# Fourteen weight splits of the output projection are taken from VectorE and given to transfers that GpSimd issues

## The chip, the cores and the metric

The kernel runs on one NeuronCore of a Trainium2 chip. The metric is the device time of one execution in microseconds (us). Before the change it was 1078.8 us, the median of two runs (1078.34 and 1079.26).

## The reference

One layer of a streaming encoder on 512 frames of 2048 columns. A combined input projection feeds two groups of heads, an RWKV-7 scan (16 heads of 64) and an HGRN2 recurrence (8 heads of 128). Their gated outputs are put side by side and go through one output projection, and a LayerNorm closes the layer:

```
proj   = x @ w_in                                  # 512 x 2048 by 2048 x 8320
o_rwkv = group_norm(rwkv7_scan(...)) ... * silu(z)  # 512 x 1024
o_hgrn = rms_norm(hgrn2_chunkwise(...)) * silu(z)   # 512 x 1024
y      = concat([o_rwkv, o_hgrn]) @ w_out           # 512 x 2048 by 2048 x 2048
out    = layer_norm(ALPHA * x + y) * ln_w + ln_b
```

The change touches only how the weights of the product with `w_out` are made ready.

## The kernel before, in words

**Products of two parts.** Every large product is made from float32 numbers that are cut in two. The high part is the number rounded to the short format of TensorE's fast pass (float32r), the low part is what is left. One product is then three matmuls: high by high, low by high and high by low (`three`, L426). `split` (L390) makes the parts: ScalarE writes the high part with an `ACTIVATE` copy, then VectorE subtracts it from the raw number and writes the low part.

**The output projection.** The 2048 output columns are taken in four blocks `d` of 512. A block runs over 16 contraction steps of 128 rows. The weights of one step, 128 partitions by 512 columns (256 KB in float32), are a *quarter*. For each quarter the four row tiles `t` of the output take three matmuls each, so a quarter keeps TensorE for twelve matmuls. Blocks 0 and 1 go through `rows`, blocks 2 and 3 through code of their own. The left operands `gh`, `gl` (tiles `xh`, `xl`) are the split gated head outputs. While block 0 runs, the last two HGRN2 heads are still being finished, and their matmuls (tile `mix`, L317 and L321) stand between the matmuls of the quarters. In block 1 only quarters are left.

**Buffers.** Raw weights come from `w_all` in halves, two quarters in one transfer of 512 KB that SyncE issues (`load`, L405) into one of two `wr` buffers. A new half is asked for once both quarters of the half two places before are split. High parts live in three `wh` buffers and low parts in three `wl` buffers. So quarter j+2 can be made ready as soon as TensorE has used up quarter j-1, that is when quarter j begins; and it must be ready when quarter j+2 begins.

**The order of the work.** The program is written by a planner at build time (`Plan`). Every operation is an `Op` with an engine, an estimated cost, and the tiles that it reads and writes. Queues of generators are pumped between matmuls, and the planner's clock decides which comes next. What comes out is one fixed order for each engine; at run time each engine goes through its own list in order, and semaphores hold an instruction until what it needs is there. `ready(i, home)` makes the split of quarter i and queues it; `part` holds TensorE's program until the planner's clock says that the low part is there. GpSimd (POOL) does little in this part of the program: four small power operations (`rsqrt`, L372) on `sm` and `rs`, for the heads.

Of the kernel before, what the change touches and what calls it, by code (L numbers as in the profile page):

```python
# [7 lines left out]
F32 = mybir.dt.float32  # L8
F32R = mybir.dt.float32r
U8 = mybir.dt.uint8  # L10
AF = mybir.ActivationFunctionType
ALU = mybir.AluOpType
# [222 lines left out]
def mixer_kernel(ctx, tc, head, x_r, w_all, par, up, ln_wb, consts, hmask, out):  # L235
    nc = tc.nc
    pe, sc_e, dve, pool = nc.tensor, nc.scalar, nc.vector, nc.gpsimd
# [17 lines left out]
    plan = Plan({**BUFS, **PBUFS})  # L255
    tags = {}

    def st(tag, shape, dt=F32):
        return spool.tile(shape, dt, tag=tag, name=nm(tag), bufs=BUFS[tag])
# [67 lines left out]
    def act_way(o, i, f, scale=1.0, bias=0.0):  # L327
        cost = 0.09 + size(o) * 0.00085 + moved(o, i) + (0.06 if isinstance(scale, bass.AP) else 0.0)
        if f == AF.Copy:
            return "act", cost, lambda: sc_e.activation(o, i, f, scale=scale)  # L330
        return "act", cost, lambda: sc_e.activation(o, i, f, scale=scale, bias=bias)  # L331

    def act(o, i, f, scale=1.0, bias=0.0):
        return Op([act_way(o, i, f, scale, bias)], [i], [o], SETS.get(f))
# [4 lines left out]
    def tt(o, a, b, f=ALU.mult):  # L339
        return dve_op([a, b], o, lambda: dve.tensor_tensor(o, a, b, f),  # L340
                      base=0.16 if o.shape[0] < P and size(o) == C and o.tensor.name in tags else 0.07)
# [48 lines left out]
    def split(hi, lo, raw):  # L390
        yield act(hi, raw, AF.Copy)
        yield tt(lo, raw, hi.bitcast(F32), ALU.subtract)
# [5 lines left out]
    raws, parts = {}, {}  # L398

    FIRST = 3  # L400
    nhead = 2 * FIRST
    nload = w_all.shape[0] + nhead
    QT = HALF // 2

    def load(j):  # L405
        if j < nload:
            raws[j] = st("wr", [P, HALF])
            nc.sync.dma_start(raws[j], w_all[j - nhead])
            plan.fetched(raws[j], 4 * HALF)

    whole_parts = set()

    def ready(i, home=None):

        if i < 2 * nload and i not in parts:
            parts[i] = home() if home else tuple(st(t, [P, QT], F32R) for t in ("wh", "wl"))

            def run():
                yield from split(*parts[i], raws[i // 2][:, i % 2 * QT : i % 2 * QT + QT])
                whole_parts.add(i)  # L420
                if i % 2:
                    load(i // 2 + 2)

            plan.add(splits, run())
# [16 lines left out]
    def part(i, width):  # L441

        ready(i)
        hi, lo = parts[i]
        plan.until(lambda: i in whole_parts and by_now(lo))
        return (hi.rearrange("p (k c) -> p k c", c=width), lo.rearrange("p (k c) -> p k c", c=width))
# [10 lines left out]
    def proj(u, hook=None):  # L457

        ps = main_ps()
        for j in range(4):  # L460
            if hook:
                hook(j)
            hi, lo = part(4 * u + j, P)
            for kk in range(4):
                if kk == 1:
                    ready(4 * u + j + 1)
                if kk == 2:
                    ready(4 * u + j + 2)
                k = 4 * j + kk
                three(ps, hi[:, kk], lo[:, kk], xh[k], xl[k], k == 0, k == KT - 1)  # L470
        return ps

    def rows(q, width, lh, ll, fin, order=range(KT), hook=None, tags=("main",)):

        pss = []
        per = QT // width
        for j in range(KT // per):
            if hook:
                hook(j)
            hi, lo = part(q + j, width)  # L480
            for t in range(4):
                if j == 0:
                    pss.append(main_ps(tags)[:, :width])
                if 0 < t < 3:
                    ready(q + j + t)
                sl = slice(t * P, t * P + P)
                for kk in range(per):
                    n = j * per + kk
                    k = order[n]
                    three(pss[t], lh[k][:, sl], ll[k][:, sl], hi[:, kk], lo[:, kk], n == 0, n == KT - 1)  # L490
                if j == KT // per - 1:
                    fin(t, pss[t])

    nunit = [0]

    def unit(n=1):
        u = nunit[0]
        nunit[0] += n
        return u
# [739 lines left out]
    for name, j in _order()[1:]:  # L1239
        if name == "i":  # L1240
# [7 lines left out]
            def fin(t, ps, ia=ia, j=j, used=used):  # L1248
                def run():
                    if t == 0:  # L1250
                        yield room(ia=1)
                        ia.append(take("ia", [P, 4, T]))
                    yield copy(ia[0][:, t], ps)
                    drop(ps)
                    if t == 3:
                        for S in HS[4 * j : 4 * j + 4]:
                            S.update(i=ia[0], used=used)

                plan.add(evacs, run())
# [140 lines left out]
    def ahead(j, d):  # L1400

        if d == 0:
            split_gated(j + 2)
            if j == 8:
                plan.until(room(big=1))
                lnw.append(take("big", [P, 2, D]))
                nc.sync.dma_start(lnw[0], ln_wb[None].to_broadcast([P, 2, D]))
                plan.fetched(lnw[0], 8 * D)
        if 0 <= j - KT // 2 - 3 < 4:
            residual(j - KT // 2 - 3, d)  # L1410

    banks = ("main", "acc", "mix")
    for d in range(2):
        rows(4 * unit(4), T, gh, gl, lambda t, ps, d=d: fin(t, ps, d), korder, lambda j, d=d: ahead(j, d),
             banks if d else banks[:1])
# [7 lines left out]
    def home(n):  # L1423
        if n < 10:
            return lambda: tuple(take("t", (P, QT), F32R) for _ in range(2))
        if n == 10:
            return lambda: tuple(take("ksq", (P, QT), F32R) for _ in range(2))
        if n < 13:
            def both():
                if not homes:  # L1430
                    homes["ia"] = take("ia", (P, 4, QT), F32R)
                return homes["ia"][:, 2 * (n - 11)], homes["ia"][:, 2 * (n - 11) + 1]

            return both
# [7 lines left out]
    for j in range(KT):  # L1442
        ahead(j, 2)
        hi, lo = part(q0 + seq.index((2, j)), T)
# [9 lines left out]
    for t in range(4):  # L1454
        sl = slice(t * P, t * P + P)
        ps = main_ps(banks)
        for n, k in enumerate(korder):
# [4 lines left out]
            hi, lo = part(q0 + seq.index((3, n)), T)  # L1462
# [81 lines left out]
```

## Time and profile before

| | before |
|---|---|
| median of two runs | 1078.8 us |
| the profiled execution | 1079.05 us |
| its span, first to last instruction | 1077.2 us |
| mean granted TensorE clock | 0.996 |
| TensorE busy | 1064.5 us, 99% of the span |
| VectorE busy | 771.2 us, 72% |
| ScalarE busy | 456.8 us, 42% |
| GpSimd busy | 63.7 us, 6% |

The profile is of one execution. PE is TensorE, PEld its weight loads, DVE is VectorE, ACT ScalarE, POOL GpSimd, SP SyncE. Matmuls overlap in the pipeline, so a matmul is listed with some 390 ns although the next starts 227 ns after it; the pace is read from the starts. In a row of the timeline the columns are start in us, duration in us, engine, line, operation, output and inputs (numbers of buffers left out), tile sizes, count, and in brackets the idle time before it and what ended it. In a row of transfers the columns are output and input, issuing queue, operation, count, size and the median time from issue to landing.

### The profile page before, as it was taken

Reading aid. Unit: us, or ns where it says so; the run is one execution under the profiler, and the core shown is the slowest. Engines: PE = TensorE matmul, PEld = TensorE weight load, DVE = VectorE, ACT = ScalarE, POOL = GpSimd, SP = SyncE. Lnnn points to the kernel's source line nnn. Section 1 sums busy time; section 2 is a strip of 40 time slices with the busy share of each in tenths; the row PEclk is TensorE's granted clock in tenths of the full one; section 3 lists DMA queues with packets and bytes.
Section 4 is the critical chain, followed back from the end, with each engine's and each line's share of the span. In section 5 each row is a group of like instructions: output and inputs, shape, how many; then the busy total and the mean of one; then the engine's idle time right before and its main releaser. Section 6 shows DMA issues by size and latency. Waiting matters only on the chain.

```text
span 1077.2 us, 18772 instructions
## 1 busy us (share of the span) xinstructions
PE 1064.5 (99%) x7210; PEld 889.8 (83%) x7210; DVE 771.2 (72%) x1816; ACT 456.8 (42%) x1015; POOL 63.7 (6%) x145
## 2 busy tenths in 40 slices
PE   9999999999999999999999999999999999999995
PEld 7888888888888888888888888888888888888884
DVE  6478978776679678787986776566976887625456
ACT  6443354544332456444236353434346564323321
POOL 0001000010000000011000001001000001000000
PEclk9999999999999999999999999999999999999998
DMA  8222321222323222123332223233332244545613
GB/s 324 62 90 78 98 80 61 63 91 89 108 75 108 87 69 76 55 93 98 92 99 61 79 60 93 89 82 105 89 98 60 61 147 153 175 122 166 204 60 127
DMA packets 34937, 108.47 MB, mean 101 GB/s; under 512 B 4128, under 2 KB 5664, under 8 KB 34720
## 3 DMA queue, kind: packets, MB, share of 16 engines
q1 hardware_dynamic: 34704, 107.08, 31.9%
q8 instruction: 57, 0.93, 0.4%
q14 instruction: 32, 0.26, 0.1%
q10 hardware_dynamic: 144, 0.20, 0.1%
HBM read 99.92 MB, written 7.34 MB: 100 GB/s over the span
## 4 chain that ended last, share of the span: by engine, by line
PE 98%; DVE 1%; DMA 0%; ACT 0%; SPq 0%; issue 0%; DVEq 0%
PE main L431 72%; PE mix L317 10%; PE mix L431 4%; PE acc L431 4%; PE main L1153 3%; PE acc L317 3%; PE mix L321 3%; PE main L317 1%; DMA q<-head 0%; DVE inv L349 0%; DVE inv L340 0%; SPq L1123 0%; DVE stats L1376 0%; ACT xh L330 0%; DVEq L1540 0%
## 5 line engine op out<-in xcount | busy, mean ns | idle before, releaser
L431 PE MATMUL main<-xh,wh 128*128 128x512 f32 x864 | 342.6, 397 | 0.0
L431 PE MATMUL main<-xl,wh 128*128 128x512 f32 x864 | 342.1, 396 | 0.0
L431 PE MATMUL main<-xh,wl 128*128 128x512 f32 x864 | 341.7, 396 | 0.0
L330 ACT ACTIVATE wh<-wr 128x512 fp32r<-128x512 f32 x299 | 186.6, 626 | 204.2 <-PE main L431 159.5
L340 DVE TENSOR_TENSOR wl<-wr,wh 128x512 fp32r<-128x512 f32 x299 | 203.9, 683 | 85.0 <-ACT wh L330 83.4
L431 PEld LDWEIGHTS main<-xh,wl 128*128 128x128 f32 x864 | 162.5, 188 | 32.2
L431 PEld LDWEIGHTS main<-xl,wh 128*128 128x128 f32 x864 | 162.6, 188 | 31.9
L431 PEld LDWEIGHTS main<-xh,wh 128*128 128x128 f32 x864 | 162.6, 188 | 31.5
L431 PE MATMUL main<-wh,xl 128*128 128x512 f32 x256 | 102.4, 400 | 0.0
L431 PE MATMUL main<-wh,xh 128*128 128x512 f32 x256 | 101.5, 396 | 0.0
L431 PE MATMUL main<-wl,xh 128*128 128x512 f32 x256 | 101.3, 396 | 0.0
L330 ACT ACTIVATE z<-mix 64x64 f32<-64x64 f32 (+1 forms) x153 | 35.9, 235 | 66.7 <-PE mix L317 27.3
L431 PEld LDWEIGHTS main<-wl,xh 128*128 128x128 f32 x256 | 48.2, 188 | 9.5
L431 PEld LDWEIGHTS main<-wh,xl 128*128 128x128 f32 x256 | 48.2, 188 | 9.1
L431 PEld LDWEIGHTS main<-wh,xh 128*128 128x128 f32 x256 | 48.2, 188 | 9.0
L331 ACT ACTIVATE t<-main,om 128x512 f32<-128x512 f32 x33 | 22.4, 688 | 73.6 <-PE main L431 64.0
L382 DVE COPY z<-mix 64x64 f32<-64x64 f32 (+1 forms) x167 | 37.8, 226 | 17.1 <-PE mix L317 8.2
L349 DVE SCALAR_TENSOR_TENSOR bd<-mix,pc,bd 64x64 f32<-64x64 f32 x112 | 31.3, 283 | 20.7 <-PE mix L317 15.0
L340 DVE TENSOR_TENSOR inv<-inv,inv 64x30 f32<-64x30 f32 (+14 forms) x120 | 38.6, 322 | 3.8 <-DVE inv L340 0.5
L349 DVE SCALAR_TENSOR_TENSOR t<-main,pr,t 128x511 f32<-128x511 f32 x33 | 24.3, 745 | 23.5 <-ACT t L331 23.3
L340 DVE TENSOR_TENSOR inv<-inv 64x30 f32<-64x30 f32 (+14 forms) x120 | 38.5, 321 | 2.9
L340 DVE TENSOR_TENSOR t<-t,tot 128x256 f32<-128x256 f32 x96 | 37.7, 415 | 0.3
(228 smaller groups left out, 1469.0 us busy)
## 6 DMA issues: line engine op xcount, KB each, us to landing
wr<-w_all SPq DMA_DIRECT2D x156, 512.0 KB, 3.6
q<-head SPq DMA_DIRECT2D x15, 448.0 KB, 5.6
g<-x_r SPq DMA_DIRECT2D x16, 256.0 KB, 3.9
spill<-g SPq DMA_DIRECT2D x12, 256.0 KB, 3.1
out<-q SPq DMA_DIRECT2D x12, 256.0 KB, 2.6
t<-spill SPq DMA_DIRECT2D x11, 256.0 KB, 4.0
big<-ln_wb SPq DMA_DIRECT2D x1, 2048.0 KB, 9.2
up<-up SPq DMA_DIRECT2D x8, 128.0 KB, 2.1
```

Of the source, the lines that this page charges most:

```text
L317: return Op([("pe", cost, lambda: pe.matmul(o, l, r, start=start, stop=stop, **kw))], [l, r], [o], mode="narrow" if narrow else "main" if ...
L321: return Op([("pe", 0.11, lambda: pe.transpose(o, i, ident))], [i], [o])
L330: return "act", cost, lambda: sc_e.activation(o, i, f, scale=scale)
L331: return "act", cost, lambda: sc_e.activation(o, i, f, scale=scale, bias=bias)
L340: return dve_op([a, b], o, lambda: dve.tensor_tensor(o, a, b, f), base=0.16 if o.shape[0] < P and size(o) == C and o.tensor.name in tags e ...
L349: return dve_op([a, b], o, lambda: dve.scalar_tensor_tensor(o, a, s, b, f1, f2), per=0.00113, base=0.085 if o.shape[0] == P else 0.25 if s ...
L382: f = lambda: dve.tensor_copy(o, i)
L431: pe.matmul(ps, l, r, start=first and i == 0, stop=last and i == 2)
L1153: pe.matmul(pss[a], *ops, start=k == 0 and low == of == 0, stop=k == KT - 1 and low == 1)
```

## The change

Two new ways of making the parts of a quarter stand beside `split`. Both use transfers that GpSimd issues (`transfer`), since such a transfer can round to float32r, or add what it moves to what lies at its destination.

- `split_added`, in block 0, quarters 3, 5, ... 15: ScalarE writes the high part from the raw tile as before. ScalarE then also writes the *negated* high part into the low tile. A GpSimd transfer adds the raw tile to it: raw minus high is the low part. VectorE does nothing.
- `split_moved`, in block 1, quarters 3, 5, ... 15: a GpSimd transfer fetches the quarter from `w_all` and rounds it into the high tile. ScalarE writes the negated high part into the low tile. A second GpSimd transfer fetches the quarter from `w_all` again and adds it. The raw tile's half with this quarter is still loaded, but not read.

```diff
+    def transfer(o, i, **kw):
+
+        yield Op([("pool", 1.0, lambda: pool.dma_start(o, i, **kw))], [i], [o])
+        plan.ready[o.tensor.name] = plan.busy[o.tensor.name] = (plan.clock["pool"] + 2.5, "dma")
+
+    def split_added(hi, lo, raw):
+
+        yield act(hi, raw, AF.Copy)
+        yield act(lo, raw, AF.Copy, scale=-1.0)
+        yield from transfer(lo, raw, accum_op=ALU.add)
+
+    def split_moved(hi, lo, src):
+
+        yield from transfer(hi, src)
+        yield act(lo, hi.bitcast(F32), AF.Copy, scale=-1.0)
+        yield from transfer(lo, src, accum_op=ALU.add)
+
+    by_transfer = {}
+
     def ready(i, home=None):
...
             def run():
-                yield from split(*parts[i], raws[i // 2][:, i % 2 * QT : i % 2 * QT + QT])
+                c = slice(i % 2 * QT, i % 2 * QT + QT)
+                how = by_transfer.get(i, split)
+                yield from how(*parts[i], w_all[i // 2 - nhead, :, c] if how == split_moved else raws[i // 2][:, c])
                 whole_parts.add(i)
...
+    for d, how in ((0, split_added), (1, split_moved)):
+        for i in range(3, 16, 2):
+            by_transfer[4 * (nunit[0] + 4 * d) + i] = how
```

The planner writes these operations into each engine's list. On ScalarE, in block 1, the list held one high part after another, each from a raw tile (`wr`); the numbers tell the buffers apart. These are quarters 0 to 5 of block 1 before:

```order
852 L330 ACTIVATE wh_9748<-wr_9683 128x512
853 L330 ACTIVATE wh_9774<-wr_9683 128x512
854 L330 ACTIVATE wh_9798<-wr_9729 128x512
855 L330 ACTIVATE wh_9819<-wr_9729 128x512
856 L330 ACTIVATE wh_9837<-wr_9780 128x512
857 L330 ACTIVATE wh_9853<-wr_9780 128x512
```

And the same six quarters now:

```order
859 L330 ACTIVATE wh_9755<-wr_9689 128x512
860 L330 ACTIVATE wh_9781<-wr_9689 128x512
861 L330 ACTIVATE wh_9805<-wr_9736 128x512
862 L330 ACTIVATE wl_9827<-wh_9826 128x512
863 L330 ACTIVATE wh_9845<-wr_9787 128x512
864 L330 ACTIVATE wl_9862<-wh_9861 128x512
```

From quarter 3 on every other row is a negated high part (`wl` from `wh`), and its input is not a raw tile but the tile that a GpSimd transfer fills.

GpSimd's list in this part of the program held four power operations, two on `sm` and two on `rs`, with nothing between them. Before, from the end of its earlier work to the first of the closing LayerNorm:

```order
140 L372 TENSOR_TENSOR sm_9193<-sm_9193,mhalf 128x8
141 L372 TENSOR_TENSOR sm_9372<-sm_9372,mhalf 128x8
142 L372 TENSOR_TENSOR rs_9441<-rs_9441,mhalf 128x4
143 L372 TENSOR_TENSOR rs_9600<-rs_9600,mhalf 128x4
144 L372 TENSOR_TENSOR rs_10498<-mv_10497,mhalf 128x1
```

Now, from the adding transfer of quarter 5 of block 0 into block 1 (`wl` from `wr` is an adding transfer of block 0, `wh` from `w_all` a rounding and `wl` from `w_all` an adding transfer of block 1):

```order
143 L415 DMA wl_9437<-wr_9315 128x512
144 L372 TENSOR_TENSOR rs_9450<-rs_9450,mhalf 128x4
145 L415 DMA wl_9510<-wr_9386 128x512
146 L372 TENSOR_TENSOR rs_9579<-rs_9579,mhalf 128x4
147 L415 DMA wl_9585<-wr_9452 128x512
148 L415 DMA wl_9639<-wr_9515 128x512
149 L415 DMA wl_9684<-wr_9604 128x512
150 L415 DMA wl_9731<-wr_9644 128x512
151 L415 DMA wh_9826<-w_all 128x512
152 L415 DMA wl_9827<-w_all 128x512
153 L415 DMA wh_9861<-w_all 128x512
154 L415 DMA wl_9862<-w_all 128x512
```

Each power operation on `rs` now stands ahead of an adding transfer: the second one ahead of the transfer of quarter 9 (`wl_9585`).

On TensorE only block 0 is in another order: matmuls of the last head stand at other places between the quarters. The row of seven that ends in `rs` stood behind the third matmul of quarter 8 (`wh_9543`):

```order
3947 L431 MATMUL main_9322<-wh_9543,xh_9558 128x512
3948 L431 MATMUL main_9322<-wl_9544,xh_9558 128x512
3949 L431 MATMUL main_9322<-wh_9543,xl_9559 128x512
3950 L317 MATMUL mix_9591<-ia_6749,t_8961 128x128 x2
3951 L317 MATMUL mix_9591<-t_8425,t_8167 128x128
```

Now it stands behind the third matmul of quarter 7 (`wh_9509`):

```order
3935 L452 MATMUL main_9322<-wh_9509,xh_9524 128x512
3936 L452 MATMUL main_9322<-wl_9510,xh_9524 128x512
3937 L452 MATMUL main_9322<-wh_9509,xl_9525 128x512
3938 L317 MATMUL mix_9570<-ia_6749,t_8961 128x128 x2
3939 L317 MATMUL mix_9570<-t_8425,t_8167 128x128
```

So this step of the last head has moved one quarter ahead.

## The prediction

> **What bounds the kernel now.** I read the page's totals and its chain of waits first. The chain gives each engine's share of the path that ended last.
>
> ```profile
> span 1077.2 us, 18772 instructions
> PE 1064.5 (99%) x7210; PEld 889.8 (83%) x7210; DVE 771.2 (72%) x1816; ACT 456.8 (42%) x1015; POOL 63.7 (6%) x145
> PE 98%; DVE 1%; DMA 0%; ACT 0%; SPq 0%; issue 0%; DVEq 0%
> ```
>
> TensorE (PE) is the path. VectorE (DVE), which the change relieves, holds 1% of it, and that lies in the closing LayerNorm. So freed VectorE time is worth nothing where PE doesn't wait for it. Next, the chain in order of time where block 1 of the output projection runs; columns are start, length, work.
>
> ```profile
> 935.38 1.36 PE acc L431 x6
> 936.74 1.36 PE mix L431 x6
> ...
> 977.54 1.36 PE mix L431 x6
> 978.90 43.52 PE main L431 x192
> ...
> 1044.35 21.95 PE mix L431 x96
> ```
>
> Pieces of six matmuls follow each other every 1.36 us, and blocks 2 and 3 follow without a break. There is no gap for this change to close: it can only leave the time, or put waits into PE. To see how late the weights may be, I read PE's own timeline at quarters 0, 1 and 3 of block 1, and ScalarE's (ACT) and VectorE's beside it.
>
> ```profile
> 935.21 0.39 PE L431 MATMUL acc<-wh,xh 128*128 128x512 f32 x1
> ...
> 937.93 0.39 PE L431 MATMUL acc<-wh,xh 128*128 128x512 f32 x1
> 938.16 0.39 PE L431 MATMUL acc<-wl,xh 128*128 128x512 f32 x1
> ...
> 943.37 0.39 PE L431 MATMUL acc<-wh,xh 128*128 128x512 f32 x1
> 943.60 0.39 PE L431 MATMUL acc<-wl,xh 128*128 128x512 f32 x1
> ```
>
> ```profile
> 938.13 0.63 ACT L330 ACTIVATE wh<-wr 128x512 fp32r<-128x512 f32 x1 [2.09 <-PE mix L431]
> 940.85 0.63 ACT L330 ACTIVATE wh<-wr 128x512 fp32r<-128x512 f32 x1 [2.09 <-PE mix L431]
> ```
>
> ```profile
> 941.52 0.69 DVE L340 TENSOR_TENSOR wl<-wr,wh 128x512 fp32r<-128x512 f32 x1 [0.62 <-ACT wh L330]
> ```
>
> A quarter lasts 937.93 - 935.21 = 2.72 us. Quarter 1 begins at 937.93, and 0.20 us later (938.13) ACT is released by PE and begins the split of quarter 3, in the buffer that quarter 0 left. Quarter 3 needs its high part at 943.37, and its low part one matmul later, at 943.60. So from the release there are **943.60 - 938.13 = 5.47 us** for the low part. The split takes from 940.85 to 941.52 + 0.69 = 942.21, or 1.36 us, with 0.04 us between ACT's end and DVE's start. It has 4.1 us to spare, and this is what the change spends.
>
> **The change part by part.** Taken from VectorE: 14 subtractions of the mean in the group below. The rows under it give busy time by engine (PE, PEld, DVE, ACT, POOL) in block 0 and in block 1, then PE's granted clock and the DMA share.
>
> ```profile
> L340 DVE TENSOR_TENSOR wl<-wr,wh 128x512 fp32r<-128x512 f32 x16 | 11.1, 691 | 24.9 <-ACT wh L330 24.9
> ```
>
> ```profile
> 884.20:932.40 48.20, 48.20 (x244) 40.53 (x243) 32.73 (x61) 20.50 (x39) 5.98 (x4) 1.00 0.54 181
> ...
> 935.20:976.00 40.80, 40.80 (x181) 33.79 (x180) 14.68 (x23) 9.48 (x15) 0.00 (x0) 1.00 0.43 129
> ```
>
> 14 x 0.69 = 9.7 us of an engine that holds nothing up: worth 0. Added on ACT: 7 negated copies in block 0 at 0.63 us each, 4.4 us, beside PE, since ACT is busy 20.50 of 48.20 us there. In block 1 a copy from `wh` replaces a copy from `wr`.
>
> The unknown is how long a transfer that GpSimd (POOL) issues takes. None is in the trace. The nearest rows are SyncE's transfers: within block 1 those from HBM, over the whole run also the stores; the last row gives shortest, median and longest of the `x_r` loads.
>
> ```profile
> wr<-w_all SPq DMA_DIRECT2D x9, 512.0 KB, 3.6
> g<-x_r SPq DMA_DIRECT2D x4, 256.0 KB, 4.2
> ```
>
> ```profile
> out<-inv SPq DMA_DIRECT2D x4, 256.0 KB, 2.4
> ```
>
> ```profile
> DMA to landing us min/median/max: 2.9/3.9/4.9
> ```
>
> A transfer of 256 KB takes 2.4 to 4.9 us. For the rounding one I take 3.6, the row with the same source. For the adding one I take 4.2, the slowest median of this stretch, because it must also read what lies at its destination. The bounds for both are 2.4 and 4.9; for the adding one twice 4.2 is kept as a far end, in a rival.
>
> *Block 1, odd quarters.* The chain from the release is: rounding transfer 3.6, handoff 0.04, ACT's negated copy 0.63, handoff 0.04, adding transfer 4.2, together **8.5 us** against 5.47: 3.0 us late. This isn't paid seven times. While PE waits for quarter 3, quarter 2 is already done, so the buffers for quarter 5 are free and its chain runs on under the wait. Let quarter 1 begin at 0. Quarter 3's low part lands at 8.5 + 0.2, PE was there at 5.67. Quarter 5's chain was released at 5.64, when quarter 3 was due, and ends at 14.1; PE finishes the 11 matmuls left of quarter 3 (11 x 0.227 = 2.5) and quarter 4 (2.72) at 13.9 and needs the low part at 14.1. So quarter 5 is just in time, and quarter 7, released at 13.9, is late again by 3.0. Late are 3, 7, 11 and 15: **4 x 3.0 = 12.1 us**, with the figure 3.03 unrounded. POOL's list allows it: the adding transfer of quarter 3 is issued at about 4.5, ahead of the rounding one of quarter 5 at 5.6. Even quarters keep their 4.1 us to spare, and behind ACT's wait stands only the high part of an even quarter, about 1.5 us late of these. DMA is 43% busy in this stretch (row above) and gains 512 KB per 5.44 us.
>
> The Trainium skill gives a price of its own. "DMA: Bandwidth & Descriptors", section "Anatomy of one DMA — SWDGE (gpsimd) path", fits a GpSimd transfer by 2.0 us plus bytes over 436,000 per us, 2.6 us for 256 KB; by that estimate the chain is 5.9 us, 0.4 late, and the sum 1.8 instead of 12.1 us. The rows from HBM in this stretch are 1.0 and 1.6 us longer, and I stay with them; no run so far shows such a transfer.
>
> *Block 0, odd quarters.* Here the raw tile is there, and two ACT copies come first. Their pace is in these rows.
>
> ```profile
> 897.30 0.62 ACT L330 ACTIVATE wh<-wr 128x512 fp32r<-128x512 f32 x1
> 897.82 0.62 ACT L330 ACTIVATE xh<-t 128x512 fp32r<-128x512 f32 x1
> ```
>
> 0.52 + 0.62 + 0.04 + 4.2 = 5.4 us, just inside 5.47: no wait. The raw buffer is now held until the transfer has read it, some 4 us longer, so SyncE's next `wr` load and the `x_r` and `big` loads queued behind it start later. The load's loop is transfer landed, load 3.6, two to three ACT copies, transfer 4.2, about 10 us per four quarters, which last 10.9: hidden, with 0.9 us of cover.
>
> One quarter is different. In POOL's list the second power operation on `rs` stands ahead of the adding transfer of quarter 9, which waits behind it though its inputs are ready.
>
> ```profile
> 908.49 0.48 PE L431 MATMUL main<-wh,xh 128*128 128x512 f32 x1
> 912.03 0.60 PE L317 MATMUL mix<-ia,t 128*128 128x128 f32 x4
> 915.68 0.39 PE L431 MATMUL main<-wh,xh 128*128 128x512 f32 x1
> ```
>
> ```profile
> 915.02 0.68 DVE L340 TENSOR_TENSOR wl<-wr,wh 128x512 fp32r<-128x512 f32 x1
> 915.62 0.16 DVE L346 TENSOR_SCALAR rs<-rs 128x4 f32<-128x4 f32 x1
> ```
>
> ```profile
> 915.86 1.38 POOL L372 TENSOR_TENSOR rs<-rs,mhalf 128x4 f32<-128x4 f32 x1 [11.35 <-DVE rs L346]
> ```
>
> Its price: before, that operation starts 3.83 us after the head's matmuls (912.03), of which 0.60 is a split that no longer stands between. Those matmuls now stand behind three of quarter 7 (908.49), so at 908.49 + 0.68 = 909.17. The power operation then ends at 909.17 + 3.23 + 1.38 = 913.8, the transfer lands at 918.0, and quarter 9 (915.68) needs it at 915.9: **2.1 us**. This goes away if the planner's new order lets PE's other small work fill it, and grows if the 2 MB `big` load, now ahead of one weight load, slows it:
>
> ```profile
> big<-ln_wb SPq DMA_DIRECT2D x1, 2048.0 KB, 9.2
> ```
>
> Sum: 12.1 + 2.1 = +14.2 us. The profiled execution, 1079.05 us with a span of 1077.2, would become 1093.2, and the median of 1078.8 becomes **1093.0 us**.
>
> **The rivals.** *Hidden.* With 2.4 us for both transfers the chain is 5.5 us and nothing is late in block 1. With 2.9 us, the shortest load, it is 6.5 and 1.0 us late, four times, and quarter 9 waits 0.8: 4.9 us. Time 1079 to 1084. For it: stores of this size take 2.4. Against it: no load of 256 KB here is under 2.9, and the medians are above.
>
> *The adding transfer takes much longer*, because it reads both operands through the same engines. At 5.3 us block 1 is 4 x 4.1 = 16.6 us late; in block 0 quarters 11 and 15, where no head work stretches the quarters, are 2 x 1.0 late and quarter 9 3.2: 21.8 us, just over 2%. That is the point from which it decides. At 8.4 us, twice the load's time, block 1 costs 4 x 7.2 = 29, block 0 2 x 4.1 + 6.3: 43 us, time 1122. For it: no row bounds an addition. Against it: DMA has half its time free.
>
> *The chains don't overlap* and each odd quarter pays: 7 x 3.0 + 2.1 = 23, time 1102. POOL's and ACT's order speak against it, as worked out above.
>
> *TensorE's clock falls in the waits.* After the last matmul (chain: PE ends at 1066.3) the granted clock, the eighth figure, stays 1.00 to 1069.0 and is then half.
>
> ```profile
> 1066.40:1069.00 2.60, 0.00 (x0) 0.00 (x0) 2.46 (x7) 0.00 (x0) 0.54 (x1) 1.00 0.00 0
> 1069.00:1072.00 3.00, 0.00 (x0) 0.00 (x0) 3.00 (x7) 1.52 (x2) 0.00 (x0) 0.54 0.21 84
> ```
>
> A mean of 0.54 over 3 us puts the fall at about 1069.2, 2.9 us after the last matmul; four waits of 3.0 us are at that edge. If one quarter then runs at half clock, each wait costs 2.72 more: 14.2 + 10.9, time 1104. The Trainium skill, "TensorE: Matmul & The Clock Gate", Part 1, says that the gate looks at windows of about 3.4 us that run free of the kernel and halves the clock after an idle one; by that rule a 3.0 us wait keeps the clock, and the trace's 2.9 us only agrees roughly.
>
> *It does nothing*: excluded, since the lists show the transfers; a gain over 2% would need PE gaps that the chain doesn't have.
>
> **How the numbers follow.** Waits as worked out, adding 5 to 21 us: 0.60. Hidden: 0.17. Adding transfer over 5.3 us: 0.14. No overlap: 0.04. Clock: 0.04. A gain from something not seen: 0.01. With 4.9 us for both transfers the chain is 10.5 us: 4 x 5.0 in block 1, 2 x 0.6 and 2.8 in block 0, so 24 us and 1103, already over 2%; the first case itself goes from 1084 to 1100. The range is 1081 to 1105: it leaves out about half of the hidden case and most of the long transfers. Beyond 2%, 21.6 us, which is about what a measurement of this kernel tells from no change: slower 0.14 + 0.04 + 0.04 = 0.22, faster 0.01, within 0.77.
>
> **What would show it.** PE idle before the low part's matmul (`wl,xh`) of quarters 3, 7, 11 and 15 of block 1, ended by a transfer, 3 us each; PE at 2.72 us per quarter elsewhere in block 1. GpSimd transfers with landing times near 3.6 and 4.2. In block 0 one wait at quarter 9, behind `rs` on POOL. VectorE 9 to 10 us less busy, without effect. Wrong would be: waits at all seven odd quarters, an adding transfer far off 4.2, a granted clock under 1.00 in block 1, or no idle at all.

## The result, and the profile after

The kernel with the change takes **1109.5 us**, the median of two runs (1109.28 and 1109.67), against 1078.8 us: a ratio of 1.0284, with an interval of 1.0240 to 1.0329. It is slower by 30.7 us, where 14.2 were forecast, and lies above the forecast's range.

The page of the changed kernel first, totals and chain of waits.

```profile
span 1107.5 us, 18835 instructions
PE 1076.3 (97%) x7210; PEld 895.7 (81%) x7210; DVE 763.4 (69%) x1802; ACT 460.7 (42%) x1022; POOL 79.7 (7%) x166
PE 91%; issue 5%; DMA 2%; POOL 1%; DVE 1%; ACT 0%; DVEq 0%; POOLq 0%; ACTq 0%; SPq 0%
```

The span grew by 1107.5 - 1077.2 = 30.3 us. VectorE is 7.8 us less busy (the subtractions alone 9.6 us, other work of its a little more), and it is worth nothing. Two things stand against it. PE's share of the path has gone from 98% to 91%, so PE now waits. And PE itself is 11.8 us *busier* with the same 7210 matmuls: some of them ran slower.

Where PE waits is seen in its timeline: these are all the waits over 1 us for a split, two in block 0 (`main`, `wr`) and four in block 1.

```profile
919.16 0.50 PE L452 MATMUL main<-wl,xh 128*128 128x512 f32 x1 [2.34 <-DMA wl<-wr]
938.60 0.50 PE L452 MATMUL main<-wl,xh 128*128 128x512 f32 x1 [1.20 <-DMA wl<-wr]
954.00 0.50 PE L452 MATMUL acc<-wl,xh 128*128 128x512 f32 x1 [4.22 <-DMA wl<-w_all]
970.43 0.50 PE L452 MATMUL acc<-wl,xh 128*128 128x512 f32 x1 [3.60 <-DMA wl<-w_all]
987.05 0.50 PE L452 MATMUL acc<-wl,xh 128*128 128x512 f32 x1 [3.75 <-DMA wl<-w_all]
1003.69 0.80 PE L452 MATMUL acc<-wl,xh 128*128 128x512 f32 x1 [3.57 <-DMA wl<-w_all]
```

They are quarters 9 and 15 of block 0 and quarters 3, 7, 11 and 15 of block 1, each before the low part's matmul, each ended by an adding transfer. The brackets count from the modelled end of the matmul before. Counted by starts, less the usual pace of 0.227 us, the loss is 2.5 and 1.4 us in block 0, and 4.4, 3.8, 3.9 and 3.7 in block 1, together **15.8 us**.

The rest is in the rows that follow a wait. Here is PE behind the wait of quarter 3, and then three stretches behind it and one behind the wait of quarter 15 (columns: length; busy time of PE, PEld, DVE, ACT, POOL; PE's granted clock; DMA share; GB/s).

```profile
954.68 0.63 PE L452 MATMUL acc<-wh,xh 128*128 128x512 f32 x1
955.10 0.63 PE L452 MATMUL acc<-wl,xh 128*128 128x512 f32 x1
...
957.98 0.39 PE L452 MATMUL mix<-wh,xl 128*128 128x512 f32 x1
958.21 0.40 PE L452 MATMUL acc<-wh,xh 128*128 128x512 f32 x1
```

```profile
954.00:956.00 2.00, 2.00 (x6) 1.57 (x7) 0.00 (x0) 0.00 (x0) 0.00 (x0) 0.61 0.74 264
956.00:958.00 2.00, 2.00 (x7) 1.57 (x6) 0.00 (x0) 0.63 (x1) 0.85 (x1) 0.54 0.00 0
958.00:964.00 6.00, 6.00 (x28) 4.89 (x27) 0.69 (x1) 0.63 (x1) 0.56 (x1) 1.00 0.68 164
...
1003.60:1009.00 5.40, 5.31 (x13) 4.16 (x14) 3.42 (x6) 0.15 (x1) 0.00 (x0) 0.50 0.19 46
```

The matmuls start 0.42 to 0.43 us apart where 0.227 is the pace, and the granted clock is half. Behind quarter 3 it is half for (1 - 0.61) x 2.00 / 0.5 + (1 - 0.54) x 2.00 / 0.5 = 3.4 us. Summed over the starts, the slow matmuls cost 8.0 us more in block 1, and in block 0 3.0 us, of which 0.8 were there before the change; the 2.2 are those behind quarter 9's wait.

So the 30.3 us are made up of: waits of block 1 15.8, low clock there 8.0, waits of block 0 3.9, low clock there 2.2; together 29.9. This is a count of where the time lies. It doesn't say that each part would come back by itself; the experiments test that.

Last, the two views that price the transfers: issues in block 0 and in block 1, and the chain of quarter 7 of block 1 on its three engines. Quarter 5 begins at 960.97, which releases the chain.

```profile
wl<-wr POOLq DMA_DIRECT2D x7, 256.0 KB, 3.6
...
wh<-w_all POOLq DMA_DIRECT2D x7, 256.0 KB, 4.2
wl<-w_all POOLq DMA_DIRECT2D x7, 256.0 KB, 4.0
```

```profile
960.97 0.39 PE L452 MATMUL acc<-wh,xh 128*128 128x512 f32 x1
```

```profile
961.50 0.56 POOL L415 DMA_DIRECT2D wh<-w_all  x1 [3.51 <-PE mix L452]
966.04 0.88 POOL L415 DMA_DIRECT2D wl<-w_all  x1 [3.98 <-ACT wl L330]
```

```profile
964.98 0.63 ACT L330 ACTIVATE wl<-wh 128x512 fp32r<-128x512 f32 x1 [5.89 <-DMA wh<-w_all]
```

The steps are: 0.53 until GpSimd issues, 3.48 for the rounding transfer, 0.63 for the copy, 0.43 until GpSimd issues again, 4.39 until PE goes on. The low part is there 9.46 us after quarter 5 began, and PE was ready for it after 5.67.

Quarter 9 of block 0 needs its own look, since the prediction put its wait down to the power operation on `rs` alone. These are ScalarE's and GpSimd's rows ahead of its transfer, which is the one issued at 914.00.

```profile
911.38 0.60 ACT L331 ACTIVATE t<-mix 128x512 f32<-128x512 f32 x1 [2.62 <-PE mix L317]
...
912.39 0.62 ACT L330 ACTIVATE wl<-wr 128x512 fp32r<-128x512 f32 x1
```

```profile
912.99 1.04 POOL L372 TENSOR_TENSOR rs<-rs,mhalf 128x4 f32<-128x4 f32 x1 [8.26 <-DVE rs L346]
914.00 0.90 POOL L415 DMA_DIRECT2D wl<-wr  x1
```

ScalarE's two copies of quarter 9 stand in its list behind a copy for the last head, which waited 2.62 us for the head's matmuls. The negated copy ends at 913.01. With the 0.34 to 0.43 us that GpSimd takes behind ScalarE elsewhere, the transfer could have been issued at about 913.4, so the power operation held it for some 0.6 us. It then took 5.1 us, beside the `big` load, and landed at 919.1.

### The profile page after: what moved, and what is told of

The parts are those of the page before. It is cut to its first block, busy times and chain, and to the rows that moved or that the text cites. A ratio compares the mean times of both kernels' runs of the same rounds, so it can differ in the third digit from the quotient of the medians.

```text
span 1107.5 us, 18835 instructions
## 1 busy us (share of the span) xinstructions
PE 1076.3 (97%) x7210; PEld 895.7 (81%) x7210; DVE 763.4 (69%) x1802; ACT 460.7 (42%) x1022; POOL 79.7 (7%) x166
## 4 chain that ended last, share of the span: by engine, by line
PE 91%; issue 5%; DMA 2%; POOL 1%; DVE 1%; ACT 0%; DVEq 0%; POOLq 0%; ACTq 0%; SPq 0%
PE main L452 68%; PE mix L317 9%; PE main L1174 3%; PE acc L317 3%; PE mix L321 2%; PE mix L452 2%; PE acc L452 2%; DMA wl<-wr 1%; PE main L317 1%; POOL wl L415 0%; PE mix L1130 0%; DMA wl<-w_all 0%; DMA wh<-w_all 0%; DMA wr<-w_all 0%; POOL wh L415 0%
## 5 line engine op out<-in xcount | busy, mean ns | idle before, releaser
L340 DVE TENSOR_TENSOR wl<-wr,wh 128x512 fp32r<-128x512 f32 x285 | 194.3, 683 | 112.1 <-ACT wh L330 110.5
L330 ACT ACTIVATE wh<-wr 128x512 fp32r<-128x512 f32 x292 | 182.1, 626 | 191.1 <-PE main L452 154.0
L452 PEld LDWEIGHTS main<-wl,xh 128*128 128x128 f32 x256 | 48.7, 190 | 14.5 <-DMA wl<-wr 5.0
L375 POOL MEMSET z<- 64x128 f32 x64 | 11.8, 200 | 379.7 <-PE acc L317 351.5
```

What stands on the lines that cost most here:

```text
L375: return Op([("pool", 0.1, lambda: pool.memset(o, v))], [], [o])
L452: pe.matmul(ps, l, r, start=first and i == 0, stop=last and i == 2)
```

## The experiments

Every run also ran the kernel before on the same chip; a ratio is against that. What is shown as a diff is against the changed kernel, with `...` where lines are left out. Wherever `by_transfer` is filled in another way, the three lines removed in the first diff are removed too, and aren't shown again. Letters of the theories are those of each expectation.

**Do the two blocks add up?** First block 0 alone, then block 1 alone.

```diff
-    for d, how in ((0, split_added), (1, split_moved)):
-        for i in range(3, 16, 2):
-            by_transfer[4 * (nunit[0] + 4 * d) + i] = how
+    for i in range(3, 16, 2):
+        by_transfer[4 * (nunit[0] + 0) + i] = split_added
```

> Block 0 changed alone, block 1 as before. Theory A (the losses are TensorE's waits for late transfers, plus matmuls at half clock behind each long wait; the blocks add up): the trace of the changed kernel shows waits of 2.5 us at quarter 9 and 1.4 us at quarter 15 of block 0 and about 1.5 us of slow matmuls behind the first: +6 us, 1085 us. Rival B (block 0 costs nothing and its waits only shift work to block 1): 1079 us.

Measured 1086.1 us, ratio 1.0064 (1.0049 to 1.0079). Both waits are there again, 2.33 us at quarter 9 and 1.29 at quarter 15. The first:

```profile
919.73 0.50 PE L452 MATMUL main<-wl,xh 128*128 128x512 f32 x1 [2.33 <-DMA wl<-wr]
```

```diff
+    for i in range(3, 16, 2):
+        by_transfer[4 * (nunit[0] + 4) + i] = split_moved
```

> Block 1 changed alone, block 0 as before. Theory A: four waits of 3.7 to 4.4 us (15.8 us together) at quarters 3, 7, 11 and 15, and 8 us of matmuls at half clock behind them: +24 us, 1102.6 us. Rival B (the waits of block 1 come from what block 0 left late): clearly less, 1090 us.

Measured 1102.1 us, ratio 1.0214 (1.0199 to 1.0230), with waits of 4.12, 3.36, 4.00 and 3.61 us (15.7 counted by starts) and 7.2 us of slow matmuls behind them. The same waits come back at the same quarters, and 6.8 + 22.9 = 29.7 us is nearly the whole loss of 30.7. The blocks can be studied apart.

**Is it the overlap of the chains that spares every second odd quarter?** If quarters 5, 9 and 13 are in time only because their chains run on under the waits of 3, 7, 11 and 15, moving these four alone must cost as much as moving seven, and moving 5, 9 and 13 alone must make them wait.

```diff
+    for i in range(3, 16, 4):
+        by_transfer[4 * (nunit[0] + 4) + i] = split_moved
```

> In block 1 only quarters 3, 7, 11 and 15 go by transfer, and block 0 as before: 8 transfers instead of 14. Theory A (chains of neighbouring odd quarters run under each other's waits, so that only every second one waits): the same four waits and the same clock falls, 1102 us within 2 us of block 1 with all seven. Rival C (each moved quarter costs by itself): 4/7 of 24 us, 1092.5 us.

Measured 1101.8 us, ratio 1.0211 (1.0191 to 1.0230): as much as all seven.

```diff
+    for i in range(5, 16, 4):
+        by_transfer[4 * (nunit[0] + 4) + i] = split_moved
```

> Only quarters 5, 9 and 13 of block 1 are moved, those that did not wait in the changed kernel. Theory A (a chain takes about 9.3 us from its release against 5.47 and is hidden only where another's wait covers it): now each of the three waits, 3 x 3.8 us and about 1.8 us of low clock behind each, 17 us, 1095 to 1097 us. Rival (these quarters are in time for a reason of their own): no wait, 1079 to 1080 us.

Measured 1094.1 us, ratio 1.0139 (1.0124 to 1.0154). Quarters 5, 9 and 13, which never wait over 1 us in the changed kernel, now wait:

```profile
952.40 0.50 PE L452 MATMUL acc<-wl,xh 128*128 128x512 f32 x1 [3.62 <-DMA wl<-w_all]
...
968.16 0.50 PE L452 MATMUL acc<-wl,xh 128*128 128x512 f32 x1 [2.97 <-DMA wl<-w_all]
...
983.52 0.50 PE L452 MATMUL acc<-wl,xh 128*128 128x512 f32 x1 [4.19 <-DMA wl<-w_all]
```

So the chains of neighbouring odd quarters do run under each other's waits. The time is 1 us under the expectation because only two of the three waits were followed by the low clock (below).

**Which half of the chain is it?** In block 1 alone, first only the rounding transfer, with VectorE subtracting as before; then only the adding one, with ScalarE's two copies from the raw tile as in block 0.

```diff
+    def split_rounded(hi, lo, src, raw):
+
+        yield from transfer(hi, src)
+        yield tt(lo, raw, hi.bitcast(F32), ALU.subtract)
...
+    for i in range(3, 16, 2):
+        by_transfer[4 * (nunit[0] + 4) + i] = split_rounded
```

> Block 1 alone: the rounding transfer stays, but VectorE makes the low part from the raw tile, as before; the adding transfer is gone. Theory A (the chain against its 5.47 us decides): release to issue 0.3, rounding transfer 3.5 to 4.3, VectorE 0.7, together 4.5 to 5.3 us: no wait, 1079 to 1080 us. Rival E (a GpSimd transfer costs in itself, by loading the queues): 7 transfers are left of 14, half of the loss, 1090 us.

Measured 1080.0 us, ratio 1.0013 (1.0004 to 1.0022), and no wait over 0.8 us.

```diff
+    for i in range(3, 16, 2):
+        by_transfer[4 * (nunit[0] + 4) + i] = split_added
```

> Block 1 alone, made as block 0 is: ScalarE writes the high part and its negative, the adding transfer stays, the rounding one is gone. Theory A: 0.2 + 1.15 + 0.45 to issue + 4.0 = 5.8 us against 5.47: late by 0.4 us four times, too short for the clock to fall: 1080 to 1082 us. Rival E: half of the loss, 1090 us.

Measured 1083.7 us, ratio 1.0044 (1.0029 to 1.0059): 2 us over what the chain of one transfer gives. The adding transfers of block 1, and PE's larger wait:

```profile
wl<-wr POOLq DMA_DIRECT2D x7, 256.0 KB, 3.3
```

```profile
979.28 0.50 PE L452 MATMUL acc<-wl,xh 128*128 128x512 f32 x1 [2.13 <-DMA wl<-wr]
```

The adding transfer by itself is 3.3 us, no longer than a rounding one (3.7 in the run before it). It is clearly late once, when it took 7.0 us in the stretch where SyncE's `x_r` loads run; that they delayed it is argued from the place, not tried apart. This one wait was followed by half clock, 1.7 us more. So neither transfer brings the four waits alone. Two in a row do.

**Is the low clock brought by the wait?** Block 1 alone again. Sixteen matmuls into a bank that nothing reads stand ahead of quarters 3, 7, 11 and 15, so that TensorE is busy in the time of the wait.

```diff
+                if t == 0 and j % 4 == 3 and by_transfer.get(q + j) == split_moved:
+                    idle = take("main")
+                    for _ in range(16):
+                        pe.matmul(idle, lh[order[0]][:, sl], lh[order[0]])
+                    drop(idle)
...
+    for i in range(3, 16, 2):
+        by_transfer[4 * (nunit[0] + 4) + i] = split_moved
```

> Block 1 changed alone, with 16 extra matmuls on ready data, into a PSUM tile that nobody reads, ahead of quarters 3, 7, 11 and 15: 16 x 0.227 = 3.6 us of work that fits into each wait. Theory A (the slow matmuls behind a wait come from the clock that falls when TensorE is idle): the clock stays at 1.00, the waits stay, the 8 us go: 1094.6 us. Rival D (the slow matmuls come from transfers that load the memory at that time): no gain, 1102.6 us or more.

Measured 1099.6 us, ratio 1.0188 (1.0171 to 1.0205): between the two, 2.6 us better than block 1 alone where 8 was hoped for. The stretch with three of the four fillings, and the one behind it, where quarter 13 waits:

```profile
935.00:983.00 48.00, 45.78 (x198) 36.63 (x197) 8.41 (x14) 7.48 (x13) 8.45 (x12) 1.00 0.58 153
983.00:991.00 8.00, 5.82 (x19) 4.35 (x19) 0.29 (x1) 0.63 (x1) 1.38 (x3) 0.80 0.57 164
```

The clock stays full wherever the wait is filled. It falls once, behind a wait of 2.18 us at quarter 13, which wasn't filled. But the time isn't regained. The dummy matmuls take 4 x 16 x 0.227 = 14.5 us, and PE still waits 5.2 us beside them: 1.3 at quarters 3 and 11, and 1.0, 0.6 and 2.3 at quarters 5, 9 and 13, which didn't wait before. That is 19.7 us against 15.7 of waits in block 1 alone. With TensorE at full pace the quarters are asked for sooner, and the transfers don't come sooner. Part of the low clock's time was therefore hidden: it slowed PE down in time in which PE would have waited anyway. It also seems that quarters 5, 9 and 13 were in time in the changed kernel because the low clock held PE back as well.

**What does the low clock cost by itself, and from what wait on?** Here no transfer is moved to GpSimd's queue. The splits are as before, and PE waits at quarters 3, 5, ... 15 of block 1 for one, or for two, power operations of GpSimd, between two small matmuls. The diff is that of the first kernel; the second has `range(2)`.

```diff
+                if t == 0 and j in (3, 5, 7, 9, 11, 13, 15) and halt and q == halt[1]:
+                    x = halt[0]
+                    idle = take(next(b for b in ("main", "acc", "mix") if plan.free(b)))
+                    pe.matmul(idle[:, :P], ident, x)
+                    for _ in range(1):
+                        pool.tensor_tensor(x[:, :4], x[:, :4], mhalf[:, :4], ALU.pow)
+                    pe.matmul(idle[:, :P], ident, x)
+                    drop(idle)
```

> No transfer by GpSimd: all splits as in the kernel before. Instead PE is made to wait at quarters 3, 5, ... 15 of block 1, seven times, for one power operation of GpSimd on 128x4 (1.4 us in the rows), between two matmuls of 128x128 that are added for it. Wait about 1.8 us each, matmuls and turns about 0.6. Theory A (the clock falls behind a wait, from about 2.3 us on, and stays low for some 10 matmuls): pace behind the waits stays 0.227 us, 7 x 2.4 = 17, 1095 to 1096 us. Rival B (any wait, however short, brings the fall): 7 x 1.5 more, 1106 us. Rival C (the fall came from the transfers' traffic, not from the wait): as A, 1095.

Measured 1092.8 us, ratio 1.0125 (1.0108 to 1.0142): 13.6 us, 1.9 each, a little under the expectation since the operation took 1.01 us here. The wait, two of the matmuls behind it, and the granted clock over the whole block:

```profile
944.64 0.49 PE L514 MATMUL main<-t,cst 128*128 128x128 f32 x2 [1.14 <-POOL t L513]
...
945.20 0.39 PE L452 MATMUL acc<-wl,xh 128*128 128x512 f32 x1
945.42 0.39 PE L452 MATMUL acc<-wh,xl 128*128 128x512 f32 x1
```

```profile
935.00:1000.00 65.00, 56.61 (x257) 46.24 (x256) 23.66 (x38) 13.55 (x22) 7.05 (x7) 1.00 0.33 100
```

> As the run with one power operation, but with two of them one after the other, so PE waits about 3.2 us at each of seven quarters. Theory A: starts 0.427 us apart for some 10 matmuls behind most waits, 2 us each: 7 x 3.8 + 14 = 40, 1118 to 1120 us. Rival C (the fall came from the transfers' traffic): pace 0.227 us throughout, 7 x 3.8 = 27, 1105 us. Rival D (a window that runs free of the kernel must be idle as a whole): the fall comes behind some of the seven waits only, at random: 1107 to 1114 us.

Measured 1111.7 us, ratio 1.0293 (1.0277 to 1.0309). Now each wait is 2.2 to 2.3 us, and the clock falls behind all seven:

```profile
946.46 0.80 PE L514 MATMUL main<-t,cst 128*128 128x128 f32 x2 [2.23 <-POOL t L513]
...
947.91 0.63 PE L452 MATMUL acc<-wh,xl 128*128 128x512 f32 x1
948.34 0.63 PE L452 MATMUL acc<-wh,xh 128*128 128x512 f32 x1
```

```profile
946.40:949.60 3.20, 3.14 (x8) 2.58 (x9) 0.00 (x0) 0.00 (x0) 0.01 (x1) 0.50 0.54 161
```

The second run costs 18.9 us more than the first. The waits are some 1.1 us longer, 7 x 1.1 = 7.7, and the slow matmuls add 11.3 - 0.6 = 10.7, together 18.4. There is no GpSimd transfer anywhere in this kernel, so it is the wait that brings the fall and not the traffic, and it costs **1.5 us a wait**. The time is 6 to 8 us under theory A, since the waits are 2.3 us and not the 3.2 aimed at; the fall came all the same. Another execution of this kernel took 1108.4 us at a mean clock of 0.989 instead of 0.986. It has no trace; by the 3.3 us that it is shorter, an estimate, two of the seven falls were missing there.

**Is the chain late because its buffers come free late?** Block 1 alone. The chain starts when quarter o's buffers are released. If its two parts go to free tiles, it can start as early as the order allows.

```diff
+            if by_transfer.get(i) == split_moved:
+                home = lambda: tuple(take("t", (P, QT), F32R) for _ in range(2))
             parts[i] = home() if home else tuple(st(t, [P, QT], F32R) for t in ("wh", "wl"))
...
+            if by_transfer.get(q + j) == split_moved:
+                drop(*parts[q + j])
```

> Block 1 alone, all 14 transfers stay, but the odd quarters' parts lie in tiles of their own that have long been free, so that a chain doesn't wait for TensorE to leave a buffer. Theory A: the chains start early, nothing is late, 1079 to 1080 us with the same bytes moved. Rival F (the transfers are too slow for the pace, or disturb the other loads): the waits stay, 1095 us or more.

Measured 1092.7 us, ratio 1.0128 (1.0112 to 1.0145): some 9 us less than block 1 alone, but some 13 over the expectation. GpSimd's issues say why; `x2` is an adding transfer and, right behind it, the rounding one of the next odd quarter.

```profile
945.08 1.42 POOL L415 DMA_DIRECT2D t<-w_all  x2 [6.78 <-ACT t L330]
952.76 1.45 POOL L415 DMA_DIRECT2D t<-w_all  x2 [6.26 <-ACT t L330]
960.24 1.42 POOL L415 DMA_DIRECT2D t<-w_all  x2 [6.04 <-ACT t L330]
```

A pair starts every 7.5 to 7.7 us, where block 1 needs one every 5.44. The rounding transfer stands in GpSimd's list behind an adding transfer that waits for ScalarE's copy, and this copy waits for the rounding transfer before. So the loop is: issue of the rounding one behind the adding one 0.6, landing 5.7 (the median of this run), copy 0.63, handoff 0.4, together 7.3. The next run breaks this loop: each rounding transfer is issued one odd quarter earlier, ahead of that adding one.

```diff
+    def ask(i):
+        if by_transfer.get(i) == split_moved:
+            early[i] = tuple(take("t", (P, QT), F32R) for _ in range(2))
+            plan.run(transfer(early[i][0], w_all[i // 2 - nhead, :, i % 2 * QT : i % 2 * QT + QT]))
...
     def ahead(j, d):
+        if d == 1:
+            i = 4 * (nunit[0] - 4) + j
+            if j == 0:
+                ask(i + 3)
+            ask(i + 4)
...
```

> As the run with tiles of their own (block 1, all 14 transfers, free tiles), but the rounding transfer of each odd quarter is issued two odd quarters ahead, so that in GpSimd's list it no longer stands behind an adding transfer that waits for ScalarE. Theory H (what held that run at 1092.7 us was the order of GpSimd's list: the rounding transfer behind the adding one of the quarter before, so that a pair could start only every 7.4 us): no wait over 1 us is left, 1079 to 1082 us. Rival I (the queue itself cannot do more: two transfers of 256 KB in 7.4 us, 3.7 us each, where block 1 asks for one every 2.72 us): waits of 2 to 3 us stay at four or more quarters, 14 times about 1 us, 1088 to 1093 us.

Measured 1079.25 us, ratio 1.0000 (0.9990 to 1.0009). All fourteen transfers are there and no wait is left. The transfers, and PE's stretch:

```profile
t<-w_all POOLq DMA_DIRECT2D x14, 256.0 KB, 6.9
```

```profile
935.00:978.00 43.00, 43.00 (x191) 35.57 (x191) 11.07 (x18) 10.93 (x18) 8.88 (x12) 1.00 0.72 196
```

They take *longer* than in any other run, 6.9 us (two are issued one behind the other, beside SyncE's loads), and it costs nothing. What the change lost in block 1 was therefore not the transfers' length and not the queue's capacity. It was how late they are asked for: by the buffers' release, and by the list.

**Is quarter 9 of block 0 late because of the power operation ahead of it?** Block 0 alone, with quarter 9 left to VectorE.

```diff
+    for i in (3, 5, 7, 11, 13, 15):
+        by_transfer[4 * nunit[0] + i] = split_added
```

> Block 0 alone, with quarter 9 split as before, so that no transfer stands behind the second power operation on rs. Theory A: the wait of 2.5 us at quarter 9 and 1.5 us of slow matmuls go; of block 0's +6 us about 2 are left: 1081 us. Rival G (quarter 9 only shows a lateness of the loads that would show elsewhere): 1084 us or more.

Measured 1084.0 us, ratio 1.0047 (1.0032 to 1.0062): 5.2 us over the kernel before, against 6.8 with quarter 9, where about 2 was expected. Quarter 15's wait went too, but a new one came, at quarter 11:

```profile
924.56 0.50 PE L452 MATMUL main<-wl,xh 128*128 128x512 f32 x1 [2.02 <-DMA wl<-wr]
```

The transfer of quarter 11 was issued at 918.37 and took 6.1 us, beside the 2 MB `big` load of 9.3 us. In block 0 with quarter 9 this load was issued at 909.06, here at 913.93 and behind a weight load:

```profile
913.54 0.33 SPq L408 DMA_DIRECT2D wr<-w_all  x1
913.93 0.43 SPq L1428 DMA_DIRECT2D big<-ln_wb  x1
```

So leaving out quarter 9 also changed the order of SyncE's list, and the run can't tell what the power operation costs by itself. The rows of quarter 9 above are the better evidence, and they give it about 0.6 of the 2.5 us.

## Why the prediction was wrong

**Right, by its own steps.** VectorE's 9.7 us (9.6 measured) were worth nothing. The path got waits into PE, ended by adding transfers. The adding transfer of block 1 was taken as 4.2 us and the median is 4.0; ScalarE's copy was 0.63. In block 1 the waits stand at quarters 3, 7, 11 and 15 and nowhere else, and two runs show that overlap is the reason. That the overlap sufficed is partly luck: the sum had quarter 5 just in time at full clock with chains of 8.5 us, and with the longer chains that were measured it was late as soon as the clock stayed full (1.0, 0.6 and 2.3 us at quarters 5, 9 and 13 in the run with dummy matmuls).

**Quarter 9 of block 0 came near by luck.** It was priced at 2.1 us and cost 2.5. The step "its inputs are ready" was wrong: ScalarE's negated copy ended at 913.01, when the power operation had just begun, because ScalarE's list held it behind the head. The power operation accounts for about 0.6 us, and the transfer took 5.1 us instead of 4.2. On the other side, PE was ready for the low part at 916.7 and not at 915.9.

**The rival that was dismissed was true: TensorE's clock.** It was given 0.04, on the step "four waits of 3.0 us are at that edge", from one fall in the tail, 2.9 us after the last matmul. The fall came behind all four waits of block 1 and behind the 2.3 us of quarter 9. The slow matmuls are 8.0 + 2.2 = 10.2 us, a third of the loss and, by count, most of what the forecast missed. This is not what a full clock would save: filling the waits of block 1 gave back 2.6 us. The rival's price, 10.9 us, came near by luck, since it is four falls of 2.72 us where five of 1.6 to 2.6 us came, six windows of 3.41 us at half clock. The step failed because one fall, 2.9 us after the last matmul, was read as the length that a wait must have. It showed only that a wait of 2.9 us can be enough; the last section works out when a shorter one is enough.

**The chain in block 1 was mis-sized.** 8.5 us from its release, or 8.71 from the beginning of the quarter that releases it, became 9.46 for quarter 7 and 10.05 for quarter 3. GpSimd was taken to start 0.20 us after that beginning, from a row of PE to ACT, and started after 0.53. The handoff from ScalarE to GpSimd was taken as 0.04 us, from a row of ACT to DVE, and was 0.43. Together that is 0.7 us more. The rounding transfer was taken as 3.6 us; its median is 4.2. So a wait is 3.7 to 4.4 us and not 3.0, and four of them 15.8 instead of 12.1.

**The steady quarters of block 0 had almost no margin.** They were costed at 0, with a chain of 5.4 us against 5.47. Quarter 15 waited 1.4 us. The handoff to GpSimd was 0.34 us instead of 0.04, which alone uses the margin up. The transfer was issued at 933.27, just behind the following loads, and landed after 5.3 us instead of 4.2.

```profile
931.40 0.33 SPq L408 DMA_DIRECT2D wr<-w_all  x1
931.83 0.85 SPq L1411 DMA_DIRECT2D g<-x_r  x2
```

The prediction had named the `big` load as a risk to quarter 9, not the `x_r` loads at the block's end. That these made the transfer slow is argued from the times; it was not tried apart.

**The other rivals.** *Hidden* is excluded by the waits. *No overlap* is excluded by the runs with four and with three quarters. *An adding transfer that takes much longer* is excluded: alone it takes 3.3 us. The estimate of 2.6 us for 256 KB by the Trainium skill's fit in "DMA: Bandwidth & Descriptors", section "Anatomy of one DMA — SWDGE (gpsimd) path", is under every median here (3.3 to 6.9), and the sum of 1.8 us by it doesn't hold.

Counted in the trace, the terms are 15.8 + 2.5 + 1.4 of waits and 10.2 of low clock, 29.9 us against 30.3 in the span. The waits alone, 19.7 us, would have been inside the forecast's range.

## What to carry to other kernels

A chain that replaces a short one must be held against the time from the release of its buffers to the need, with every handoff at its own engine's price; where it doesn't fit, ask for its first link earlier, in a buffer of its own and at a place in the issuing engine's list where nothing waits ahead of it, and here even 7 us transfers cost nothing. A wait on a TensorE at full pace should be priced at its length alone up to 1.8 us, at its length plus 1.5 to 2 us of low clock from about 3.75 us on, and by its chance of lying mostly in one window of the clock between these (worked out below). What a full clock would give back is less where the next transfers would be late anyway. And where the freed engine isn't on the path, the best to hope for is the time before: the run of block 1 without waits gave exactly that.

## What the runs showed of the hardware that was not expected

**TensorE's clock is set window by window, and a window need not be idle throughout to halve it.** In the changed kernel the falls of the granted clock begin at 920.29, 954.42, 971.49, 988.56 and 1002.21, read in stretches of 0.02 us. These times are 34.13, 17.07, 17.07 and 13.65 us apart, which is 10, 5, 5 and 4 times 3.41 us. Each low stretch lasts 3.41 us, the last one twice that. So the clock changes only at points that are 3.41 us apart, wherever a wait begins or ends: it fell 0.4 us behind the wait of quarter 3, and 1.5 us ahead of the end of quarter 15's. What decides is how idle the window before such a point was. The wait of quarter 11 lies across two windows (second column length, third PE's busy time):

```profile
981.73:985.14 3.41, 1.57 (x7) 0.95 (x6) 0.69 (x1) 1.00 (x2) 1.43 (x2) 1.00 0.33 31
985.14:988.56 3.42, 1.51 (x7) 1.25 (x8) 0.00 (x0) 0.00 (x0) 0.00 (x0) 1.00 1.02 304
988.56:991.97 3.41, 3.41 (x10) 2.63 (x9) 0.37 (x1) 1.26 (x2) 0.86 (x1) 0.50 0.36 130
```

Behind 3.41 - 1.57 = 1.84 us of idle time the clock stayed full, behind 3.42 - 1.51 = 1.91 us it was halved. The same holds in all fourteen traces up to the last matmul, with the windows laid by each trace's own falls and the idle time by the modelled ends of the matmuls. No window at full clock with up to 1.84 us of idle time was followed by half clock, and all 25 with 1.91 us or more were. The length of a wait decides only through this. The 2.97 us of the run with three quarters fell into two windows, and the clock stayed full:

```profile
963.49:966.90 3.41, 1.70 (x8) 1.08 (x6) 1.39 (x2) 1.68 (x3) 0.86 (x1) 1.00 0.32 44
966.90:970.31 3.41, 2.15 (x9) 1.80 (x10) 0.00 (x0) 0.00 (x0) 0.00 (x0) 1.00 0.84 242
```

Waits of 2.57 us (free tiles) and 3.20 us (four quarters) were split between two windows in the same way and brought no fall. The 2.13 us of the run with the adding transfer, and all seven waits of the run with two power operations, gave one window at least 2.08 us of idle time and did. A wait of 3.0 us, as predicted, keeps the clock only if neither window gets more than about 1.87 us of it; by an estimate, that is so for 2 x 1.87 - 3.0 = 0.74 us of the 3.41 us in which it can begin, so the chance of a fall was near 0.8 for each wait.

The Trainium skill, "TensorE: Matmul & The Clock Gate", Part 1, tells of an activity window of about 3.4 us that runs free of the kernel; the 3.41 us here and the fixed points agree with that. The section puts the fall behind an idle window of that length; here windows with up to 1.51 us of work in them were enough.

**GpSimd picks up work slowly.** From the end of ScalarE's copy to the adding transfer's issue it takes 0.43 us (965.61 to 966.04), where ACT to DVE took 0.04. An issue is listed with 0.55 to 1.05 us, and where a second one stood right behind it, it began 0.6 to 0.9 us after the first (949.79 and 950.40, 966.04 and 966.97).

**An addition costs a transfer nothing that shows.** In block 1 of the changed kernel, both from `w_all`, the median was 4.0 us for the adding and 4.2 for the rounding transfers. Alone it was 3.3 from a raw tile, against 3.7 for a rounding one from `w_all`, but there the sources differ.
